# A hybrid decoder step on one core: DVE's queue in program order, a third buffer for projected tiles, one buffer for gate and square

## Chip, core, metric

One core of a Trainium2 chip. The metric is the device time of one execution in microseconds (us). Engines: PE (TensorE; PEld is its weight load), DVE (VectorE), ACT (ScalarE), POOL (GpSimd), SP (SyncE, which issues most transfers).

## What is computed

One layer of a decoder with two parallel groups of eight heads, all in float32, for 512 new tokens of a prompt and for 8 sequences with 4 new tokens each (32 tokens), so T = 544 columns in all. Cut to what matters:

```python
p = einsum('btd,de->bte', rmsnorm(x), w_in)          # 2048 -> 8192 columns
qa, ka, va, za, qb, fb, ib, zb = split(p)            # 1024 columns each
# group A, per head: stick-breaking attention; causal means s < t
z = qa @ ka.T * scale + bias
log_1m = where(causal, log_sigmoid(-z), 0)
tail = reverse_cumsum(log_1m) - log_1m
o_a = where(causal, exp(log_sigmoid(z) + tail), 0) @ va
# group B, per head: gated linear recurrence
g = lb + (1 - lb) * sigmoid(fb)
S_t = diag(g_t) S_{t-1} + (1 - g_t) ib_t^T ;  o_b_t = S_t^T silu(qb_t)
# both
m = concat(head_rmsnorm(o_a) * silu(za), head_rmsnorm(o_b) * silu(zb))
y = rmsnorm(x + m @ w_out)
```

The 8 sequences attend besides to 2048 cached positions each, in pages of 128, and start group B from a stored state. Keys, values and states of the new tokens are outputs too.

## The kernel before

**Product with split weights.** Each float32 weight piece (128 x 1024 values) is loaded by SP, rounded by ACT (`whi`, L259) and its remainder taken by DVE (`wlo`, L260). `project` (L381) multiplies a column block of 128 by all tokens in three products (hi x hi, hi x lo of the tokens, lo x hi), 96 matmuls for two pieces, into two PSUM banks (the whole pool `ps_acc`), one for each half of the tokens. At the end DVE empties each half into a tile in SBUF (L408). The next projection begins in the bank of the first half. These tiles come from `atile` (L924), with AT buffers.

**Order of the work.** `Flow` (L76) decides while the program is written: the base work is the sequence of projections, in portions of four matmuls; between portions it inserts side work (attention, decoding of pages, recurrence) from generators, each of which names the cost of its next step, the delay until it may come, and how long it holds one of three PSUM banks (`GBANKS`, `gbank`). The delays and the hold are numbers written by hand. When a step is inserted, its instructions for all engines are issued, so that the program has one order in which each engine's instructions stand. Under `manual_schedule` (L164) PE and SP keep that order in their queues. The queues of DVE, ACT and POOL are put in order by the scheduler of the framework, which lets an instruction pass others that it believes to be waiting still; once built, each queue is fixed.

**Stages.** Token tiles are transposed and split first (`prep_tokens`); at portion 23 of the first projection that is over (L944) and the pools for the rest are opened. Then come the eight query projections of group A; then `group_a`: for each head K, V and gate projections, with `attend` (L455) of the head beside the gate's projection. In `attend`, for each of four token blocks (512, 384, 256 and 128 columns): a score matmul into a bank (zp, L462); DVE empties it (L464); POOL masks the diagonal (L465); then `stick_sums`:

```python
nc.scalar.activation(lt[:, :n], z[:, :n], AF.Exp)                     # L447
nc.scalar.activation(lt[:, :n], lt[:, :n], AF.Ln, bias=1.0)           # L448
nc.vector.scalar_tensor_tensor(lt[:, :n], z[:, :n], GUARD, lt[:, :n], # L449
                               ALU.max, ALU.min)
nc.vector.tensor_tensor_scan(...)                                     # L450
nc.vector.tensor_tensor(z[:, :n], z[:, :n], lt[:, :n], ALU.subtract)  # L452
```

After the four blocks PE transposes K and V into banks (knp, vnp, and kvsp for the 32 new tokens), which ACT (L478) and DVE (L487, L489) empty; later steps transpose the weights of attention (wp) and multiply them by V (op). `gate` (L411) computes a sigmoid in three ACT passes (L217 to L219) and two products on DVE (L413, L414). `finish_head` (L416) squares the output on POOL (L418, tile sq), sums the squares with two matmuls (L425, L426), takes the root on ACT, and scales on DVE (L429, L436); the result goes to DRAM from the buffer of sq (L437).

`decode` (L645) runs beside both groups in 36 steps: pages of keys are loaded by SP (kpage, three buffers), transposed by DVE (L550, `k_turn`, the second of a step 14 us of planned time after the first) and multiplied (dzp, L678); pages of values are multiplied by the weights (av, L688). After every fourth step the scores of a sequence go through L698 and `stick_sums`.

`group_b`: for each head the projections bq, bf, bi and, mostly behind them, bz; `hgrn` (L705) is added when bi is written. It makes operands on DVE (L711 to L717), then goes through four rounds: two pairs of score matmuls (L746), selected into att (L757 to L763 in the first round, six L803 and in one round L811 in the others), and operands for the next round (L818, L822, L779, L781). Then transposes (khp, khsp), states and outputs. At last `out_first` and `out_rest` multiply by w_out (yacc, L1106).

**Buffers that the change touches.** In `atile` two buffers serve q, K, V and gate tiles in turn, in `group_b` bq, bf, bi and bz. `hgrn` reads q (L711) only after bi was written. In group A the gate uses a tile sg of 544 columns and `finish_head` a tile sq of 512; in group B the sigmoids of `hgrn` and of the gate share a tile sgm, and sq is another.

Of the kernel before, what the change touches and what calls it, by code (L numbers as in the profile page):

```python
# [9 lines left out]
F32 = mybir.dt.float32  # L10
# [8 lines left out]
P = 128  # L19
D = 2048  # L20
NK = D // P
SEQ = 512
# [4 lines left out]
T = SEQ + NS  # L27
# [113 lines left out]
def hybrid_step(ctx: ExitStack, tc: tile.TileContext, x_prompt, x_sample, cache_k, cache_v, state_s, page_table,  # L141
# [27 lines left out]
    def gbank(name):  # L169
        return ps_g.tile([P, 512], F32, name=name, tag="g")  # L170
# [7 lines left out]
    def mm(n):  # L178
        return 4.0 * max(n, 128) / 2.4
# [31 lines left out]
    def rsqrt_mean(out, ssq, n):  # L211
        k = out.shape[0]
        nc.scalar.activation(out, ssq, AF.Ln, bias=eps[:k], scale=1.0 / n)
        nc.scalar.activation(out, out, AF.Exp, scale=-0.5)

    def sigmoid(out, x):
        nc.scalar.activation(out, x, AF.Exp, scale=-1.0)  # L217
        nc.scalar.activation(out, out, AF.Ln, bias=1.0)
        nc.scalar.activation(out, out, AF.Exp, scale=-1.0)  # L219
# [191 lines left out]
    def gate(hh, zt, sg):  # L411
        sigmoid(sg, zt)
        nc.vector.tensor_tensor(zt[:, :SEQ], zt[:, :SEQ], sg[:, :SEQ], ALU.mult)  # L413
        nc.vector.tensor_tensor(sz_s[:, hh, :], zt[:, SEQ:], sg[:, SEQ:], ALU.mult)  # L414

    def finish_head(pool, hh, ot, zt, after):  # L416
        sq = pool.tile([P, SEQ], F32, name="sq", bufs=1)
        nc.gpsimd.tensor_tensor(sq, ot, ot, ALU.mult)  # L418
        hi = pool.tile([P, SEQ], F32R, name="sqhi", bufs=1)
        lo = pool.tile([P, SEQ], F32R, name="sqlo", bufs=1)  # L420
        nc.scalar.activation(hi, ot, AF.Square)
        nc.gpsimd.tensor_tensor(lo, sq, hi.bitcast(F32), ALU.subtract)
        yield mm(512) / 2, after + 2500.0, 1500.0, 0.0
        sp = gbank("sp")
        nc.tensor.matmul(sp, ones_r, hi, start=True, stop=False)  # L425
        nc.tensor.matmul(sp, ones_r, lo, start=False, stop=True)  # L426
        rs = sq
        rsqrt_mean(rs, sp, P)
        nc.vector.scalar_tensor_tensor(rs, ot, gains[:, hh:hh + 1], rs, ALU.mult, ALU.mult)  # L429
        if hh >= KEPT:  # L430
            while dec_done[0] < DB:
                yield 0.0, 500.0, 0.0, 0.0
            m_raw[hh] = dp.tile([P, SEQ], F32, name="vpage", bufs=NV)
            nc.vector.tensor_tensor(m_raw[hh], rs, zt[:, :SEQ], ALU.mult)
        else:
            nc.vector.tensor_tensor(rs, rs, zt[:, :SEQ], ALU.mult)  # L436
            nc.gpsimd.dma_start(m_dram[hh], rs)  # L437
        m_done[hh] = True

    KEPT = 14  # L440
    OFF = 7000.0
    AT = 2
    m_done = [False] * 16
    m_raw = [None] * 16

# [9 lines left out]
    def attend(h, qt, kt, vt, res):  # L455
# [56 lines left out]
        if "zt" in res:  # L512
            yield from finish_head(ap, h, ot, res["zt"], 1500.0)
# [20 lines left out]
    def k_fetch(n):  # L534
        while len(kpending) < min(n, len(kunits)):
            t = dp.tile([P, 4, 512], F32, name="kpage", bufs=3)
            b, gp, h2 = kunits[len(kpending)]
            for i in (0, 2, 1, 3):
                src = kpages[page_value(k_held, b, gp, i), :, h2 * 512:h2 * 512 + 512]
                nc.sync.dma_start(t[32 * i:32 * i + 32], src.rearrange("o (s r) e -> (o r) s e", r=32))  # L540
            kpending.append(t)
# [161 lines left out]


    def hgrn(h, q, F, it, res):  # L705
        sg = bp_.tile([P, T], F32, name="sgm")
        sigmoid(sg, q)
        e0 = etile()
        e3 = e0[:, :3 * T // 2].rearrange("p (u x) -> p u x", x=3)
        pairs = "p (u t) -> p u t"  # L710
        nc.vector.tensor_tensor(e3[:, :, 0:2], q.rearrange(pairs, t=2), sg.rearrange(pairs, t=2), ALU.mult)  # L711
        sg = bp_.tile([P, T], F32, name="sgm")
        sigmoid(sg, F)
        nc.vector.tensor_scalar(F, sg, lb1[:, h:h + 1], lb0[:, h:h + 1], ALU.mult, ALU.add)
        f2 = F.rearrange(pairs, t=2)
# [173 lines left out]
        if finish:  # L889
            yield from finish_head(bp_, H + h, ot, res["zt"], 1500.0)  # L890
# [33 lines left out]
    def atile(name):  # L924
        return tp_.tile([P, T], F32, name=name, tag="at", bufs=AT)

    def group_a():
        nonlocal ap, dp, tp_, later, earlier
        for h in range(H):
            if h == H - 1:  # L930
                k_fetch(3)
            if h == 2:
                for c in (slice(0, 6 * P), slice(6 * P, NM * P)):
                    lvlf = ap.tile([P, 6 * P], F32, name="lt", tag="lvlf", bufs=1)[:, :c.stop - c.start]
                    nc.gpsimd.dma_start(lvlf, masks[:, c])
                    nc.gpsimd.tensor_copy(lvls[:, c], lvlf)
            qts = []

            def qtile():
                qts.append(atile("qt"))  # L940
                return qts[0]

            for i, c in enumerate(project(qtile, h * P, h == 0)):
                if h == 0 and i == 23:  # L944
                    flow.wait(lambda: not flow.side)
                    xstack.close()
                    dp = dstack.enter_context(tc.tile_pool(name="dpool", bufs=1))
                    dcon = dp.tile([P, C_TOT - C_LATER], F32, name="dcon")
                    nc.sync.dma_start(dcon, consts[:, C_LATER:])
                    later, earlier = dcon[:, :P], dcon[:, P:]  # L950
                    tp_ = dstack.enter_context(tc.tile_pool(name="tpool", bufs=1))
                    lvls = tp_.tile([P, NM * P], U8, name="lvls")
                    lvl.extend(lvls[:, P * i:P * i + P] for i in range(NM))
                    ap = astack.enter_context(tc.tile_pool(name="apool", bufs=1))
                yield c
            nc.gpsimd.tensor_copy(q_new[:, h, :], qts[0][:, SEQ:])
            nc.gpsimd.dma_start(q_dram[h], qts[0][:, :SEQ])
        flow.add(decode(H / 64, STOP), 2)
        for h in range(H):
            qt = ap.tile([P, SEQ], F32, name="ql", bufs=2)  # L960
            nc.sync.dma_start(qt, q_dram[h])
            kt = atile("kt")
            yield from project(kt, W + h * P)
            vt = atile("vt")
            yield from project(vt, 2 * W + h * P)
            res = {}
            flow.wait(lambda: not a_side or a_side[-1] not in flow.side)
            a_side.append(flow.add(attend(h, qt, kt, vt, res), 0))
            zt = atile("zt")
            yield from project(zt, 3 * W + h * P)  # L970
            sg = ap.tile([P, T], F32, name="sg")
            gate(h, zt, sg)
            res["zt"] = zt
            if "ot" in res:
                a_side.append(flow.add(finish_head(ap, h, res["ot"], zt, 4500.0), 0))
# [31 lines left out]
    def group_b():  # L1007
        ress = [{} for _ in range(H)]

        def heads(h):  # L1010
            q = atile("bq")
            yield from project(q, 4 * W + h * P)
            F = atile("bf")
            yield from project(F, 5 * W + h * P)
            if h:
                flow.wait(lambda: hg_done[h - 1])
            if not h:
                open_b()
            it = atile("bi")
            yield from project(it, 6 * W + h * P)  # L1020
            flow.add(hgrn(h, q, F, it, ress[h]), 0)

        def gates(h):
            zt = atile("bz")
            yield from project(zt, 7 * W + h * P)
            sg = bp_.tile([P, T], F32, name="sgm")
            gate(H + h, zt, sg)
            ress[h]["zt"] = zt
            if "ot" in ress[h]:
                flow.add(finish_head(bp_, H + h, ress[h]["ot"], zt, 4500.0), 0)  # L1030

        for h in range(H - 1):
            yield from heads(h)
            if h < H - 2:
                yield from gates(h)
        yield from heads(H - 1)
        for c in gates(H - 2):
            load_m()
            yield c
        flow.wait(lambda: merged)  # L1040
        load_m()
        flow.add(mix_first, 1)
        yield from gates(H - 1)

    def load_m():
        if dec_done[0] < DB or not all(m_done[:KEPT]) or m_raw[0] is not None:
            return
        for k in (0, 4):
            t = dp.tile([P, 4, 512], F32, name="kpage", bufs=3)
            nc.sync.dma_start(t, m_dram[k:k + 4].rearrange("k p t -> p k t"))  # L1050
            for j in range(4):
                m_raw[k + j] = t[:, j, :]
        for k in range(8, KEPT):
            m_raw[k] = dp.tile([P, SEQ], F32, name="vpage", bufs=NV)
            nc.sync.dma_start(m_raw[k], m_dram[k])
# [213 lines left out]
```

## Time and profile before

| | us |
|---|---|
| timed runs, median of 2 | 1408.0 (1407.3 and 1408.7) |
| the profiled execution | 1405.46 |
| its span, first to last instruction | 1403.8 |
| PE busy | 1331.7 |
| DVE busy | 758.3 |
| ACT busy | 413.6 |
| POOL busy | 311.7 |

The span is the time between the first and the last instruction that the profiler recorded; the execution takes 1.7 us more. Busy time is the union of an engine's instructions. Matmuls are pipelined, so PE's busy time is not PE at its peak. In a row, "a <-b" behind a number tells what ended the idle time before an instruction.

### The profile page before, as it was taken

The numbers are of one execution on the slowest core, as the hardware profiler recorded it, in microseconds if no ns is written. First come the engines' busy times: TensorE is split into PE (matmuls) and PEld (weight loads), VectorE is DVE, ScalarE is ACT, GpSimd is POOL, SyncE is SP. The second block draws the span as 40 slices with busy tenths as digits, with TensorE's granted clock in tenths as the row PEclk, the third lists the DMA queues.
The fourth block names the chain that finished last, engine by engine and source line by source line (L and its number), as shares of the span: only waits on it lengthen the run. The fifth ranks groups of instructions, "written<-read, shape, count | busy, mean of one in ns | idle before, by whom it ended". The sixth has DMA issues, their size and how long they took to land.

```text
span 1403.8 us, 30662 instructions
## 1 busy us (share of the span) xinstructions
PE 1331.7 (95%) x11922; PEld 1215.2 (87%) x11922; DVE 758.3 (54%) x1302; ACT 413.6 (29%) x701; POOL 311.7 (22%) x577
## 2 busy tenths in 40 slices
PE   6999999899999999999989989999999999999997
PEld 6999888798988888888887978889899897988996
DVE  6324555647466474667575674665455658222223
ACT  6211324224233242331222231132323225222223
POOL 3212113112132121132332232121213324111001
PEclk9999999999999999999999999999999999999999
DMA  7338876699989898898888978746523251622223
GB/s 218 109 109 214 200 203 163 174 292 235 280 228 269 236 258 220 229 273 212 247 231 233 274 193 235 229 143 196 149 61 113 65 194 42 240 76 78 89 76 143
DMA packets 245027, 260.69 MB, mean 186 GB/s; under 512 B 13497, under 2 KB 169842, under 8 KB 244178
## 3 DMA queue, kind: packets, MB, share of 16 engines
q1 hardware_dynamic: 237600, 235.00, 60.5%
q0 software_dynamic: 5504, 15.80, 3.3%
q10 hardware_dynamic: 1778, 7.93, 1.5%
q8 instruction: 94, 1.54, 0.5%
q14 instruction: 51, 0.42, 0.1%
HBM read 239.15 MB, written 19.53 MB: 184 GB/s over the span
## 4 chain that ended last, share of the span: by engine, by line
PE 74%; issue 10%; DVE 9%; DMA 3%; ACT 3%; POOL 1%; SPq 0%; DVEq 0%; POOLq 0%; ACTq 0%
PE pacc L401 42%; PE yacc L1106 13%; DVE kpage L550 3%; PE av L688 3%; PE dzp L678 3%; PE sp L746 2%; DMA kpage<-in_cache_k 2%; PE op L507 1%; PE usp L897 1%; PE ysp L1115 1%; DVE wlo L260 1%; DMA wraw<-in_w_in 1%; DVE lt L450 1%; DVE att L803 1%; PE wp L174 1%
## 5 line engine op out<-in xcount | busy, mean ns | idle before, releaser
L401 PE MATMUL pacc<-h_hi,whi 128*128 128x256 f32 (+1 forms) x2048 | 546.4, 299 | 15.2 <-ACT whi L259 9.8
L401 PE MATMUL pacc<-h_lo,whi 128*128 128x256 f32 (+1 forms) x2048 | 530.4, 289 | 0.0
L401 PEld LDWEIGHTS pacc<-h_hi,whi 128*128 128x128 f32 x2048 | 389.1, 190 | 40.1 <-issue 22.9
L401 PEld LDWEIGHTS pacc<-h_lo,whi 128*128 128x128 f32 x2048 | 389.2, 190 | 1.7 <-issue 0.2
L260 DVE TENSOR_TENSOR wlo<-wraw,whi 128x1024 fp32r<-128x1024 f32 x160 | 198.0, 1240 | 199.0 <-PE yacc L1106 78.0
L259 ACT CAST whi<-wraw 128x1024 fp32r<-128x1024 f32 x160 | 166.6, 1046 | 458.3 <-PE pacc L401 312.7
L401 PE MATMUL pacc<-h_hi,wlo 128*128 128x256 f32 (+1 forms) x2048 | 294.6, 292 | 0.0
L401 PEld LDWEIGHTS pacc<-h_hi,wlo 128*128 128x128 f32 x2048 | 269.5, 189 | 13.0 <-issue 12.3
L550 DVE STREAM_TRANSPOSE kpage<-kpage 128x2048 f32<-128x2048 f32 x64 | 146.2, 2296 | 0.2 <-issue 0.2
L1106 PE MATMUL yacc<-whi,m_hi 128*128 128x256 f32 x512 | 130.4, 293 | 0.0
L1106 PE MATMUL yacc<-whi,m_lo 128*128 128x256 f32 x512 | 126.7, 285 | 3.1 <-DVE m_lo L1096 3.0
L1106 PEld LDWEIGHTS yacc<-whi,m_hi 128*128 128x128 f32 x512 | 98.8, 193 | 16.8 <-issue 13.0
L1106 PEld LDWEIGHTS yacc<-whi,m_lo 128*128 128x128 f32 x512 | 99.1, 194 | 3.6 <-DVE m_lo L1096 3.5
L678 PE MATMUL dzp<-kpage,qblk 128*32 128x128 f32 x2048 | 68.3, 281 | 23.1 <-DVE kpage L550 23.0
L678 PEld LDWEIGHTS dzp<-kpage,qblk 128*32 128x32 f32 x2048 | 54.8, 112 | 33.0 <-DVE kpage L550 27.4
L1106 PE MATMUL yacc<-wlo,m_hi 128*128 128x256 f32 x512 | 68.3, 282 | 0.0
L1178 POOL TENSOR_TENSOR y<-y,fnw 128x512 f32<-128x512 f32 (+1 forms) x18 | 26.3, 1477 | 178.7 <-DVE y L1174 111.2
L1106 PEld LDWEIGHTS yacc<-wlo,m_hi 128*128 128x128 f32 x512 | 64.3, 191 | 0.0
L688 PE MATMUL av<-vpage,dwt 128*32 128x512 f32 x512 | 62.2, 600 | 0.0
L658 POOL COPY qblk<-q_new 32x32 f32<-32x32 f32 x128 | 45.7, 357 | 31.0 <-PE dzp L678 25.8
L746 PE MATMUL sp<-bE,kr 128*128 128x192 f32 x256 | 47.4, 326 | 1.9 <-DVE o_s L596 1.4
L803 DVE COPY_PREDICATED att<-lvls,sp 128x192 f32<-128x192 uint8 (+2 forms) x144 | 38.3, 310 | 15.9 <-PE sp L746 14.9
(262 smaller groups left out, 1372.3 us busy)
## 6 DMA issues: line engine op xcount, KB each, us to landing
wraw<-in_w_in SPq DMA_DIRECT2D x128, 512.0 KB, 5.9
kpage<-in_cache_k SPq DMA_DIRECT2D x256, 256.0 KB, 5.5
vpage<-in_cache_v SPq DMA_DIRECT2D x256, 256.0 KB, 5.1
wraw<-in_w_out SPq DMA_DIRECT2D x32, 512.0 KB, 3.5
bst<-in_state_s SPq DMA_DIRECT2D x16, 256.0 KB, 6.2
out<-bst POOLq DMA_DIRECT2D x16, 256.0 KB, 3.9
y<-in_x_prompt ACTq DMA_DIRECT2D x4, 1024.0 KB, 7.4
xt<-in_x_prompt SPq DMA_DIRECT2D x7, 512.0 KB, 5.8
```

The lines of the kernel that those rows point to most:

```text
L174: nc.tensor.transpose(out, in_, ident[:k, :k])
L259: turns.append(nc.scalar.copy(hi, raws[i]))
L260: nc.vector.tensor_tensor(lo, raws[i], hi.bitcast(F32), ALU.subtract)
L401: nc.tensor.matmul(ps[half][:, :n], a[:, j, :], x[:, j, ts], start=(kh == 0 and part == 0 and r == 0), stop=(kh == 1 and part == 1 and r = ...
L550: nc.vector.transpose(flat, flat)
L658: nc.gpsimd.tensor_copy(out.rearrange("p h (g x) -> p h g x", g=4)[:, :, :, :DT], q_new[32 * j:32 * j + 32, :, DT * b:DT * b + DT].rearran ...
L678: nc.tensor.matmul(zp[32 * g:32 * g + 32, gp * P:(gp + 1) * P], qb[:, at:at + 32], kt[:, g, :, 32 * j:32 * j + 32], start=(gp == 0 and h2 ...
L688: nc.tensor.matmul(av[hf][32 * i:32 * i + 32, :], wt[:, gp, i, :], vpending[n], start=(gp == 0), stop=(gp == 3))
L746: nc.tensor.matmul(sp[:, i * 192:(i + 1) * 192], kr[:, n * P:(n + 1) * P], moving(n), start=True, stop=True)
L803: nc.vector.copy_predicated(a4[:, :, :, d * hl:], m.unsqueeze(1).to_broadcast([P, 2, u, w]), s4[:, :, :, at:at + w])
L1106: nc.tensor.matmul(out, m[4 * kq + j][:, c], b[:, j, :], start=(kq == 0 and part == 0 and r == 0 and (one or tb % 2 == 0)), stop=(kq == 3 ...
L1178: nc.gpsimd.tensor_tensor(part, part, fnw[:, cs].unsqueeze(1).to_broadcast([P, n, CG]), ALU.mult)
```

## The change

It opens a second region in which DVE, too, keeps the program's order; it begins where the token tiles are done and lasts to the end. It gives `atile` three buffers. It lets sq and the sigmoids' tiles share one buffer in each of the two groups.

```diff
     def finish_head(pool, hh, ot, zt, after):
-        sq = pool.tile([P, SEQ], F32, name="sq", bufs=1)
+        sq = pool.tile([P, T], F32, name="sq", tag="sg", bufs=1)[:, :SEQ]
         nc.gpsimd.tensor_tensor(sq, ot, ot, ALU.mult)
...
-    AT = 2
+    AT = 3
...
     def hgrn(h, q, F, it, res):
-        sg = bp_.tile([P, T], F32, name="sgm")
+        sg = bp_.tile([P, T], F32, name="sgm", tag="sg")
         sigmoid(sg, q)
...
-        sg = bp_.tile([P, T], F32, name="sgm")
+        sg = bp_.tile([P, T], F32, name="sgm", tag="sg")
         sigmoid(sg, F)
...
                     xstack.close()
+                    ctx.enter_context(tc.manual_schedule(engines={mybir.EngineType.DVE}))
                     dp = dstack.enter_context(tc.tile_pool(name="dpool", bufs=1))
...
         def gates(h):
...
-            sg = bp_.tile([P, T], F32, name="sgm")
+            sg = bp_.tile([P, T], F32, name="sgm", tag="sg")
             gate(H + h, zt, sg)
```

## Rows read from the trace of the kernel before

**Rows 1.** The page, part 1: busy us, share, instructions.

```profile
PE 1331.7 (95%) x11922; PEld 1215.2 (87%) x11922; DVE 758.3 (54%) x1302; ACT 413.6 (29%) x701; POOL 311.7 (22%) x577
```

**Rows 2.** Windows: stretch, length, busy by engine (instructions), PEclk, DMA share, GB/s.

```profile
150.00:570.00 420.00, 390.32 (x3817) 354.05 (x3816) 249.45 (x358) 139.99 (x256) 86.22 (x168) 0.98 0.85 229
570.00:920.00 350.00, 332.27 (x3276) 297.94 (x3278) 222.56 (x412) 89.95 (x139) 85.98 (x192) 0.99 0.84 231
920.00:1175.00 255.00, 251.43 (x1929) 232.62 (x1917) 144.04 (x341) 72.34 (x102) 68.06 (x135) 0.99 0.42 127
```

**Rows 3.** Waits of PE: line, whom for, us in total, times, longest.

```profile
PE dzp L678 <- DVE kpage L550: 23.0, 15, 3.4
PE pacc L401 <- ACT whi L259: 9.8, 4, 3.5
...
PE knp L174 <- DVE z L464: 2.8, 2, 1.9
PE pacc L401 <- DVE zt L408: 2.4, 1, 2.4
```

**Rows 4.** Timeline of DVE, third head of group A: start, us, instruction, [idle before].

```profile
265.80 0.75 DVE L464 TENSOR_SCALAR z<-zp,sbb 128x512 f32<-128x512 f32 x1 [1.76 <-PE zp L462]
268.34 0.69 DVE L449 SCALAR_TENSOR_TENSOR lt<-z,lt 128x512 f32<-128x512 f32 x1 [1.79 <-ACT lt L448]
269.07 1.23 DVE L450 TENSOR_TENSOR_SCAN lt<-ones_r,lt 128x512 f32<-128x512 f32 x1
270.33 0.69 DVE L452 TENSOR_TENSOR z<-z,lt 128x512 f32<-128x512 f32 x1
270.93 1.22 DVE L260 TENSOR_TENSOR wlo<-wraw,whi 128x1024 fp32r<-128x1024 f32 x1
```

**Rows 5.** Groups by line and shape, 150 to 570 us: busy, mean ns | idle.

```profile
L464 DVE TENSOR_SCALAR z<-zp,sbb 128x128 f32<-128x128 f32 x8 | 2.7, 343 | 0.0
L450 DVE TENSOR_TENSOR_SCAN lt<-ones_r,lt 128x128 f32<-128x128 f32 x8 | 3.2, 398 | 0.0
...
L447 ACT ACTIVATE lt<-z 128x512 f32<-128x512 f32 x8 | 5.0, 630 | 78.9 <-POOL z L465 78.9
L447 ACT ACTIVATE lt<-z 128x128 f32<-128x128 f32 x8 | 2.4, 295 | 0.0
```

**Rows 6.** Timeline, second head of group A, DVE and PE.

```profile
207.88 0.61 DVE L464 TENSOR_SCALAR z<-zp,sbb 128x384 f32<-128x384 f32 x1
...
208.54 0.71 PE L174 MATMUL knp<-cst,kt 128*128 128x128 f32 x4 [1.93 <-DVE z L464]
```

**Rows 7.** Timeline, first and last head of group A: first L464 and kvsp.

```profile
154.14 0.75 DVE L464 TENSOR_SCALAR z<-zp,sbb 128x512 f32<-128x512 f32 x1 [1.35 <-PE zp L462]
...
159.67 0.27 PE L174 MATMUL kvsp<-cst,kt 128*32 128x128 f32 x1
...
556.66 0.75 DVE L464 TENSOR_SCALAR z<-zp,sbb 128x512 f32<-128x512 f32 x1 [1.35 <-PE zp L462]
...
560.10 0.27 PE L174 MATMUL kvsp<-cst,kt 128*32 128x128 f32 x1
```

**Rows 8.** Timeline, third head of group B, DVE, then PE.

```profile
802.69 1.45 DVE L803 COPY_PREDICATED att<-lvls,sp 128x192 f32<-128x192 uint8 x6
...
813.10 0.69 DVE L449 SCALAR_TENSOR_TENSOR dc<-dz,dc 128x512 f32<-128x512 f32 x1 [1.36 <-ACT dc L448]
...
815.69 2.30 DVE L550 STREAM_TRANSPOSE kpage<-kpage 128x2048 f32<-128x2048 f32 x1
...
805.09 0.35 PE L401 MATMUL pacc<-h_hi,whi 128*128 128x256 f32 x1 [0.56 <-DVE bz L408]
...
813.21 1.46 PE L746 MATMUL sp<-bE,kr 128*128 128x192 f32 x8
...
819.79 0.91 PE L174 MATMUL khp<-cst,kr 128*128 128x128 f32 x4 [2.67 <-DVE att L803]
```

**Rows 9.** Windows: a stretch of the second head of group A.

```profile
200.00:225.00 25.00, 20.64 (x191) 18.68 (x189) 19.45 (x29) 9.96 (x22) 12.88 (x26) 0.93 0.82 207
```

## The prediction

> **What bounds the kernel now.** I read the page first. PE is busy for 1331.7 us of a span of 1403.8, 95% [rows 1], so whatever PE loses is lost by the kernel, and whatever it cannot lose is safe. DVE is busy for about half of the time. Cutting the span into stages [rows 2] shows where PE's 72 us of idle time lie: 29.7 in the attention stage (420 minus 390.32, from 150 to 570 us), 17.7 in the recurrent stage while cached pages are still read (350 minus 332.27), 3.6 in the rest of that stage; start and end hold most of what is left. The waits of PE [rows 3] give the causes: 23.0 us for key pages that DVE has not yet transposed, 9.8 for weights that ACT has not yet rounded, 2.8 and 2.4 for a PSUM bank and an accumulator that DVE has not yet emptied. All of it is order on DVE and ACT, none of it their total work. So at most some 45 us can be won (29.7 + 17.7, less what has other causes), and the question is whether the program's order serves PE better than the planner's.
>
> **What changes on DVE.** No operation is added or removed. Before, DVE's queue was ordered by the scheduler, which let an instruction pass others that were waiting. Afterwards each DVE instruction stands exactly where the Python code issues it. That hurts where the code issues a chain that leaves DVE for ACT and comes back: DVE now waits out the round trip.
>
> **Term 1, attention: four chains one behind another.** For every head, attend issues per token block one score matmul into a PSUM bank, then on DVE L464 (which empties the bank), L449, L450 and L452, with POOL and two ACT passes between L464 and L449. Four blocks of 512, 384, 256 and 128 columns follow one another. In one head of before the first chain happened to run unmixed [rows 4]: L464 at 265.80, L449 only at 268.34 after 1.79 us idle, and the next DVE instruction at 270.93. So one chain of 512 columns holds DVE for 5.2 us. A chain of 128 columns is shorter by 0.41 on L464 and 0.83 on L450 (0.75 and 1.23 [rows 4] against 0.343 and 0.398 [rows 5]), by twice 0.335 for the ACT passes (630 against 295 [rows 5]) and, as an estimate, by as much as L464 on L449 and on L452: 5.2 minus 2.7 is 2.5. In thirds between: 4.3 and 3.4.
>
> There are three banks for such work. The fourth score matmul takes the first chain's bank, then the transposes knp, vnp and kvsp take the banks of chains 2, 3 and 4, which are free when the L464 of each is done. That this is a real wait is seen in [rows 6]: knp began at 208.54 after 1.93 us idle, right after the second L464 (207.88 plus 0.61). In program order those L464 end at 5.2 + 0.6 = 5.8, at 5.2 + 4.3 + 0.5 = 10.0 and at 5.2 + 4.3 + 3.4 + 0.3 = 13.2 us after the first one starts. PE does not pass a waiting instruction, so kvsp starts 13.2 us after the first L464. In before it starts 5.5 us after it in the first head (159.67 minus 154.14) and 3.4 in the last (560.10 minus 556.66) [rows 7]; over the eight heads 5.5, 9.3, 10.1, 3.5, 3.5, 3.9, 3.4 and 3.4, in all 42.6. The loss is 8 x 13.2 minus 42.6 = 63 us. In the first two heads a wait for rounded weights of about 2.5 us comes just after (part of the 9.8 of [rows 3]) and now falls into the longer one: 58. Bounds: 0, if DVE's slack took it all, and 85, if POOL and ACT make each chain a fifth longer (8 x 2.7 more). I take 58, since the chain and the bank wait are both rows of this kernel.
>
> A rule of the Trainium skill speaks the other way here (Perfetto Trace Analysis, Optimizing Tensor Performance): independent matmul groups should rotate through PSUM banks, so that emptying one overlaps the next. By it three banks cover this and term 1 is nothing, which would take the sum below from 1495 to 1437. The row with 1.93 us shows the rotation already stopping PE in before.
>
> **Term 2, the recurrent heads.** Here the chain of a round is: scores on PE, six L803, then L818, L822, L779 and L781, which make the operands of the next round. Before, the scheduler put some of these last ones, the emptying of an accumulator (L408) and a key transpose ahead of others. I walked one head in program order with the durations of [rows 8]. PE issued the first scores of the round at 801.31, so L803 can start at 802.05; with six L803, L811, L818 (0.68), L822, L779 and L781 (0.5, 0.4, 0.3) ahead of it, L408 ends at 806.5 and PE resumes there, not at 805.09: 1.5 us. Then come the transpose (2.3), L408's other half (0.4), three ACT passes for the gate (2.1) with DVE waiting, L413 and L414 (0.8), a weight remainder L260 (1.2, [rows 4]), L803 and the four operand makers (3.4): ready at 816.7. PE has 8.1 us of work from its resumption to the third round (813.21 minus 805.09) and wants it at 814.7: 2 more. If a decode chain stands behind it (L698 to L452, 4.8 us with 1.36 idle), then another transpose (2.3), six L803, L818 and L822 (2.7), khp starts at 826.4 and not at 819.79: 6.6 us for that head. Without the decode chain the sum is 1.5 + 2 = 3.5. Four heads have pages beside them: 4 x 5 = 20. In the last four there is no transpose; the same walk gives 1.9 for L408 alone and 3 with the gate, two heads each: 10. Term 2 is 30. Bounds: minus 5 (the 3.6 us of idle there and little more, if everything fits) and 60 (two such waits per head).
>
> **Term 3, what is won.** A key transpose that the scheduler moved behind chains now stands where the code has it. Of the 23.0 us [rows 3] I give back half, 12; bounds 0 and 23.
>
> **Term 4, the clock.** After idle time PE ran for a while at half speed: 0.93 granted over 25 us [rows 9] is 3.5 us at 1.2 instead of 2.4 GHz, which costs 1.7 us. Six such stretches lie in 150 to 920 us. With gaps of 3.8, 3.2 and 2.7 us in every attention head I add four there and two later: 11 us with the lost work of the longer ones. Bounds 0 and 25.
>
> **The two other edits.** Three buffers instead of two for projected tiles: with DVE in program order the third tile of a recurrent head could not be written before q is read, and q is read behind it, so two would not do. It shortens nothing that PE waits for: no wait of PE for such a tile's reader is in [rows 3]. One buffer for gate and square: the square of a head (POOL) waits for the gate's last reader, and a sigmoid waits for the store of the head before. The planner puts the matmul that needs the square 7 us behind the gate, more than the wait; without that cover it would cost a round trip like the 1.79 of [rows 4] for up to sixteen heads, 29 us. I take 0.
>
> **Sum.** The profiled execution took 1405.5 us; 58 + 30 - 12 + 11 = 87 more is 1492.5. The median of the timed runs is 2.5 us above that execution: 1495.
>
> **Rivals.**
> - Attention alone pays, DVE's slack swallows term 2: 58 - 12 + 8 = 54 more, 1462. For it: DVE is free for half of the recurrent stage. Against: its operands are made in a chain.
> - ACT starves PE as well: the rounding of the next weights sits in ACT's queue behind the last chain's exponentials, and PE waits another 4 us in every attention head: 32 more, 1527. For it: the 9.8 us of [rows 3] arose so.
> - It is faster: the order costs nothing because PE finds a free bank, and late transposes, unrounded weights and clock losses go. All of them (23.0 + 9.8 + 2.8 + 2.4 and six times 1.7) are 48; half is 24: 1384. It decides if knp starts within some 2 us of the first L464, as it did in five heads. Against it stands the program's own order.
> - It makes no difference, because DVE is not what limits: 1408. A reorder of an engine with 46% of its time free would then be absorbed. This is the Trainium skill's rule (Perfetto Trace Analysis, Identifying the Most-Contended Engine): work on the engine with the highest occupancy first; by it DVE at 54% moves nothing.
> - It doesn't do what it says, because the region opened inside the outer one ends PE's and SP's own order; no row prices that.
>
> **Chances and range.** The forecast 0.50, attention alone 0.20, ACT too 0.14, faster 0.07, no difference 0.07, not as said 0.02 (put with no difference). About 2%, 28 us, can be told from no change. So slower 0.84, within 2% 0.09, faster 0.07. The range goes from 1430 (attention alone with half of term 1: 1408 + 29 - 12 + 4) to 1560 (ACT too, with term 1 at its upper bound: 1527 + 27, and a little more); the forecast's own is 1460 to 1530.
>
> **What would show it.** Right: in every attention head DVE runs L464, L449, L450, L452 four times over with 1 to 2 us idle in each; PE waits for L464 before knp, vnp and kvsp, some 9 us a head and 60 or more in all; PE's idle time between 150 and 570 us roughly triples; L408 and L822 appear among PE's waits in the recurrent stage; the wait for key transposes shrinks. Wrong: knp within 2 us of the first L464, or PE's wait for L464 staying under 10 us in all, or a recurrent stage as dense as before.

## The result: 9% slower, and the profile after

The changed kernel takes 1538.5 us (median of two runs, 1535.4 and 1541.6) against 1408.0: 1.093 times the time of before, 95% interval 1.083 to 1.102. Slower was forecast and the time lies in the range, but the forecast was 87 us more and it is 130. The profiled execution took 1541.6 us, its span is 1539.9. Lines of the changed kernel behind L947 are one higher than before.

Part 1 of the page after, which answers to [rows 1]:

```profile
PE 1381.2 (90%) x11922; PEld 1252.5 (81%) x11922; DVE 776.2 (50%) x1302; ACT 423.5 (28%) x701; POOL 303.8 (20%) x577
```

The instructions are the same in number. PE's idle time went from 72.1 us (1403.8 minus 1331.7) to 158.7, by 86.6; and PE is *busy* for 49.5 us longer with the same matmuls. So the 136 us have two parts, and the second is not a wait.

Windows of the changed kernel by stage: attention (from the first emptying of a key tile to that of the first bq), the recurrent heads (to the last bz), the end. Columns as in [rows 2].

```profile
139.60:675.60 536.00, 454.21 (x4155) 409.26 (x4154) 273.34 (x376) 159.27 (x271) 83.01 (x172) 0.91 0.72 195
675.60:1299.30 623.70, 573.22 (x4939) 518.21 (x4941) 358.65 (x737) 152.38 (x223) 146.95 (x322) 0.96 0.62 172
1299.30:1539.90 240.60, 224.24 (x1817) 198.95 (x1816) 85.53 (x102) 68.82 (x147) 41.24 (x28) 0.95 0.31 108
```

The same three stages of the kernel before, cut at its own marks:

```profile
139.30:595.10 455.80, 426.12 (x4154) 388.05 (x4153) 268.16 (x375) 148.74 (x270) 91.08 (x172) 0.99 0.85 230
595.10:1173.50 578.40, 557.78 (x4940) 507.07 (x4942) 351.82 (x738) 153.10 (x224) 149.30 (x324) 0.99 0.66 186
1173.50:1403.80 230.30, 219.63 (x1816) 195.45 (x1810) 79.35 (x102) 68.73 (x147) 37.61 (x27) 0.98 0.33 113
```

Attention pays 80.2 us, of which 52.1 idle (81.8 minus 29.7) and 28.1 more busy time; the recurrent heads 45.3, of which 29.9 idle and 15.4 busy; the end 10.3 (5.7 and 4.6). The granted clock fell from 0.99 to 0.91 and 0.96, and that is the longer busy time: up to PE's last matmul, the clock record of the trace of before has 9 stretches at 1.2 GHz, 37.5 us in all, that of the changed kernel 27, 160.4 us in all. PE was busy for 35.8 and 124.6 us of them. Half of the 88.8 us more is 44, of the 49.5 (an estimate: work at half speed taken to last twice as long).

The waits of PE in the changed kernel's attention stage, then in its recurrent stage; they answer to [rows 3]:

```profile
PE knp L174 <- DVE z L464: 28.5, 8, 4.1
PE dzp L678 <- DVE kpage L550: 15.6, 4, 6.2
PE pacc L401 <- DVE kt L408: 12.0, 2, 9.5
PE pacc L401 <- DVE vt L408: 6.3, 1, 6.3
...
PE sp L746 <- DVE bE L781: 12.0, 5, 4.9
PE khp L174 <- DVE kr L822: 9.7, 4, 4.3
PE pacc L401 <- DVE bz L408: 8.8, 7, 1.9
```

Every one of these is a wait for DVE, which is busy half of the time. What DVE itself waits for, first after, then before:

```profile
DVE wlo L260 <- ACT whi L259: 118.6, 26, 10.0
...
DVE lt L449 <- ACT lt L448: 63.7, 32, 4.5
```

```profile
DVE wlo L260 <- ACT whi L259: 25.0, 10, 4.7
...
DVE lt L449 <- ACT lt L448: 6.1, 8, 1.8
```

The 32 waits at L449 are the 8 x 4 chains of term 1. The 118.6 us at L260 stand in no term: the code writes the low part of a weight piece (L260) a piece ahead, and DVE stops there until ACT has rounded it, with all that is due behind it. The scheduler had placed it where the wait was short.

The clearest place is at 464 us, DVE's timeline of the changed kernel:

```profile
464.34 1.23 DVE L260 TENSOR_TENSOR wlo<-wraw,whi 128x1024 fp32r<-128x1024 f32 x1 [9.51 <-ACT whi L259]
465.48 0.74 DVE L429 SCALAR_TENSOR_TENSOR sq<-ot,vecs,sq 128x512 f32<-128x512 f32 x1
...
468.97 0.69 DVE L449 SCALAR_TENSOR_TENSOR dc<-dz,dc 128x512 f32<-128x512 f32 x1 [1.36 <-ACT dc L448]
469.70 1.22 DVE L450 TENSOR_TENSOR_SCAN dc<-ones_r,dc 128x512 f32<-128x512 f32 x1
470.96 0.69 DVE L452 TENSOR_TENSOR dz<-dz,dc 128x512 f32<-128x512 f32 x1
471.57 2.30 DVE L550 STREAM_TRANSPOSE kpage<-kpage 128x2048 f32<-128x2048 f32 x1
473.79 0.38 DVE L596 TENSOR_REDUCE o_s<-detp 128x4 f32<-128x16 f32 x4
474.10 0.77 DVE L408 TENSOR_TENSOR kt<-pacc,rbc 128x256 f32<-128x256 f32 x2
```

The accumulator that PE needs was full by 464.7; it is emptied at 474.10, behind a wait for a weight, a decode chain that waits for ACT, and a page. PE's timeline at that place:

```profile
474.65 0.55 PE L401 MATMUL pacc<-h_hi,whi 128*128 128x256 f32 x1 [9.52 <-DVE kt L408]
475.00 0.41 PE L401 MATMUL pacc<-h_lo,whi 128*128 128x256 f32 x1
475.21 0.41 PE L401 MATMUL pacc<-h_hi,whi 128*128 128x256 f32 x1
...
484.34 0.28 PE L401 MATMUL pacc<-h_lo,whi 128*128 128x256 f32 x1
484.46 0.28 PE L401 MATMUL pacc<-h_hi,whi 128*128 128x256 f32 x1
```

And the windows around it, 10 us each:

```profile
465.00:475.00 10.00, 0.48 (x3) 0.38 (x2) 8.54 (x15) 1.51 (x3) 0.59 (x1) 0.76 1.04 312
475.00:485.00 10.00, 10.00 (x63) 10.00 (x63) 2.60 (x11) 2.22 (x5) 1.16 (x2) 0.73 0.38 102
485.00:495.00 10.00, 10.00 (x130) 8.19 (x129) 7.36 (x6) 1.05 (x1) 0.00 (x0) 1.00 0.36 101
```

From 475 to 485 us PE waits for nothing, but the clock is at 0.73: some 5.4 of the 10 us went by at 1.2 instead of 2.4 GHz. In them matmuls of one and the same shape start 0.21 us apart, and 0.12 us afterwards. As an estimate, 5.4 us at 0.12/0.21 of the pace lose some 2.3 us, and this gap of 9.5 us cost about 12. The counts, 63 and 130 matmuls, don't give the loss: the second stretch has 64 short ones of a key page among them, which take 2 us.

### The profile page after: what moved, and what is told of

Read it like the earlier page. It is cut to its first block, busy times and chain, and to the rows that moved or that the text cites. A ratio compares the mean times of both kernels' runs of the same rounds, so it can differ in the third digit from the quotient of the medians.

```text
span 1539.9 us, 30643 instructions
## 1 busy us (share of the span) xinstructions
PE 1381.2 (90%) x11922; PEld 1252.5 (81%) x11922; DVE 776.2 (50%) x1302; ACT 423.5 (28%) x701; POOL 303.8 (20%) x577
## 5 line engine op out<-in xcount | busy, mean ns | idle before, releaser
L401 PE MATMUL pacc<-h_hi,whi 128*128 128x256 f32 (+1 forms) x2048 | 561.9, 305 | 32.7 <-DVE kt L408 12.0
L401 PE MATMUL pacc<-h_lo,whi 128*128 128x256 f32 (+1 forms) x2048 | 543.5, 295 | 0.0
L401 PEld LDWEIGHTS pacc<-h_hi,whi 128*128 128x128 f32 x2048 | 400.8, 196 | 57.9 <-issue 46.5
L401 PEld LDWEIGHTS pacc<-h_lo,whi 128*128 128x128 f32 x2048 | 400.7, 196 | 1.9 <-issue 0.5
L260 DVE TENSOR_TENSOR wlo<-wraw,whi 128x1024 fp32r<-128x1024 f32 x160 | 204.4, 1279 | 282.3 <-ACT whi L259 118.6
L401 PE MATMUL pacc<-h_hi,wlo 128*128 128x256 f32 (+1 forms) x2048 | 298.1, 294 | 0.0
L401 PEld LDWEIGHTS pacc<-h_hi,wlo 128*128 128x128 f32 x2048 | 273.5, 192 | 14.6 <-issue 14.0
L550 DVE STREAM_TRANSPOSE kpage<-kpage 128x2048 f32<-128x2048 f32 x64 | 147.1, 2300 | 0.0
L678 PE MATMUL dzp<-kpage,qblk 128*32 128x128 f32 x2048 | 68.9, 288 | 23.4 <-DVE kpage L550 23.4
L688 PE MATMUL av<-vpage,dwt 128*32 128x512 f32 x512 | 65.6, 633 | 0.0
L746 PEld LDWEIGHTS sp<-bE,kr 128*128 128x128 f32 x256 | 43.2, 198 | 15.1 <-issue 14.2
L803 DVE COPY_PREDICATED att<-lvls,sp 128x192 f32<-128x192 uint8 x144 | 42.4, 314 | 19.3 <-PE sp L746 16.0
```

Source lines behind the costliest of these rows:

```text
L260: nc.vector.tensor_tensor(lo, raws[i], hi.bitcast(F32), ALU.subtract)
L401: nc.tensor.matmul(ps[half][:, :n], a[:, j, :], x[:, j, ts], start=(kh == 0 and part == 0 and r == 0), stop=(kh == 1 and part == 1 and r = ...
L550: nc.vector.transpose(flat, flat)
L678: nc.tensor.matmul(zp[32 * g:32 * g + 32, gp * P:(gp + 1) * P], qb[:, at:at + 32], kt[:, g, :, 32 * j:32 * j + 32], start=(gp == 0 and h2 ...
L688: nc.tensor.matmul(av[hf][32 * i:32 * i + 32, :], wt[:, gp, i, :], vpending[n], start=(gp == 0), stop=(gp == 3))
L746: nc.tensor.matmul(sp[:, i * 192:(i + 1) * 192], kr[:, n * P:(n + 1) * P], moving(n), start=True, stop=True)
```

## The experiments

The theory: in a fixed queue each instruction that waits for ACT holds back what PE is waiting for, at several separate places, and every gap on PE costs half-speed time besides. Rivals: the buffers, losses carried from one stage to the next, a wait that only moves. The stages of all kernels, from their windows as above; in each pair the first number is the length, the second PE's idle time in it (length minus PE busy), in us. The median is that of all timed runs; stages and PE busy are those of the one profiled execution, which in *attention only* was the slowest (1498.1) and in *recurrent on* the quickest (1458.0).

| kernel | median | ratio to before, 95% | attention | recurrent | end | PE busy |
|---|---|---|---|---|---|---|
| before | 1408.0 | | 455.8, 29.7 | 578.4, 20.6 | 230.3 | 1331.7 |
| changed | 1538.5 | 1.083 to 1.102 | 536.0, 81.8 | 623.7, 50.5 | 240.6 | 1381.2 |
| buffers only | 1410.2 | 1.000 to 1.004 | 459.0, 29.5 | 579.5, 22.9 | 229.9 | 1331.4 |
| attention only | 1491.2 | 1.053 to 1.063 | 539.2, 80.1 | 585.0, 22.4 | 229.8 | 1371.8 |
| recurrent on | 1466.0 | 1.037 to 1.046 | 458.0, 29.5 | 621.3, 49.3 | 237.9 | 1348.6 |
| chains held | 1500.0 | 1.061 to 1.071 | 493.9, 55.8 | 621.1, 47.9 | 240.5 | 1363.1 |
| operands first | 1529.6 | 1.084 to 1.090 | 534.3, 79.5 | 611.6, 42.2 | 240.3 | 1377.1 |
| low part later | 1494.4 | 1.059 to 1.065 | 510.4, 63.6 | 604.2, 38.8 | 237.9 | 1362.3 |
| three together | 1441.7 | 1.021 to 1.026 | 475.5, 38.3 | 590.2, 31.8 | 236.1 | 1343.0 |
| five together | 1434.9 | 1.016 to 1.024 | 469.3, 38.1 | 589.9, 27.7 | 232.9 | 1343.2 |
| five, order free | 1413.8 | 1.003 to 1.007 | 461.7, 30.3 | 579.2, 21.3 | 232.3 | 1339.0 |

**Buffers only.** The line that fixes DVE's order is left out.

```diff
-                    ctx.enter_context(tc.manual_schedule(engines={mybir.EngineType.DVE}))
```

> The two buffer edits alone: three buffers for projected tiles, gate and square in one buffer, and DVE's order left to the scheduler again, as before. Theory (DVE's fixed order costs everything): 1408 us within 0.5%, PE's idle gaps and half-speed stretches as before (63.5 us and 42.9 us). Rival (the buffers carry part of the loss: the shared buffer holds the next gate back until the head's square is done, and the third tile lets projections run ahead of the side work): 1420 us or more, with waits of ACT's sigmoid for POOL or DVE on that buffer.

Measured 1410.2, PE busy 1331.4. By themselves the buffers carry at most 0.4%; the rest of the loss comes with the line that is left out. The shared buffer does leave a wait: the sigmoids of group B (L217) wait 27.0 us in all for the store of a head's result (`m_dram`) from it, and 33.7 us in the changed kernel. PE's idle time in the recurrent stage is 2.3 us above that of before here; whether the wait costs more while DVE's order is fixed was not run.

What that line changes, the traces of this kernel and of the changed one show, by line and tile of each instruction: PE's 11922 matmuls and SP's transfers stand in the same order in both. Of DVE's 1302 instructions at least 450 stand elsewhere. So do at least 160 of ACT's 701 and 119 of POOL's 577, though their queues are still the scheduler's: it ordered them anew around DVE's. No run separates what ACT's new order adds to the waits of DVE for ACT.

**Attention only, and from the recurrent heads on.** The region is closed, or opened, just ahead of group B (`mstack` is a new `ExitStack`).

```diff
-                    ctx.enter_context(tc.manual_schedule(engines={mybir.EngineType.DVE}))
+                    mstack.enter_context(tc.manual_schedule(engines={mybir.EngineType.DVE}))
...
+    mstack.close()
     flow.run(group_b(), per=2)
```

> The changed kernel, with DVE's fixed order closed where the recurrent heads begin. Theory (each stage pays for its own queueing): the attention stage keeps its 80 us (first key tile to first recurrent query tile 536 us instead of 456), the recurrent stage is as before (about 578 us for the recurrent heads, 230 us for the end): 1408 + 80 = 1488 us. Rival (attention leaves pages and decode work late, and that is what costs the recurrent heads their 45 us): the recurrent stage is still 30 us or more longer than before, 1520 us or more.

```diff
-                    ctx.enter_context(tc.manual_schedule(engines={mybir.EngineType.DVE}))
...
+    ctx.enter_context(tc.manual_schedule(engines={mybir.EngineType.DVE}))
     flow.run(group_b(), per=2)
```

> The changed kernel, with DVE's fixed order opened only where the recurrent heads begin. Theory (each stage pays for its own): attention as before, recurrent heads +45 us, the end +10 us: 1408 + 55 = 1463 us. Rival (the recurrent loss is carried over from attention): the recurrent heads lose less than 15 us, 1420 us.

Measured 1491.2 and 1466.0. With the region closed the recurrent stage is 585.0 us long (6.6 over before), with the region opened late it is 621.3. Both rivals fall: each stage pays for itself, and the two losses, 5.8% and 4.1%, add up to that of the changed kernel (9.3%, interval 8.3 to 10.2).

**Chains held.** The second half of a chain is written one block later, behind the next block's L464; `exp_log` is the two ACT passes, `chain` what follows them, and the last block's is written behind the transposes of K.

```diff
-            stick_sums(z, lt, n)
-            nc.scalar.activation(z, z, AF.Exp)
+            exp_log(z, lt, n)
+            for due in held:
+                due()
+
+            def due(z=z, lt=lt, n=n):
+                chain(z, lt, n)
+                nc.scalar.activation(z, z, AF.Exp)
+
+            held = [due]
```

> The changed kernel, with the second half of each attention chain (max, scan, subtraction) written one block later, behind the next block's eviction of its scores, so that no eviction in DVE's queue has a chain in front of it that waits for ACT. Theory (the written order, not the fixing of it, costs the attention heads): PE's waits of the natural-key bank for L464 fall from 28.5 us to under 6, the attention stage gets shorter by these and by a share of the half-speed clock (28 of 86 us of gaps brought about 16 of 50 us): about 1495 us. Rival (the wait moves: the same chains then stand in front of the key tile, the decode chain and the pages): within 1% of 1538 us, with those waits grown by as much.

DVE's timeline in the last head of this kernel (L470 is L464 of before, L455 to L458 are L449 to L452):

```profile
589.65 1.27 DVE L470 TENSOR_SCALAR z<-zp,sbb 128x512 f32<-128x512 f32 x2
592.46 0.69 DVE L455 SCALAR_TENSOR_TENSOR lt<-z,lt 128x512 f32<-128x512 f32 x1 [1.54 <-ACT lt L448]
...
595.06 0.48 DVE L470 TENSOR_SCALAR z<-zp,sbb 128x256 f32<-128x256 f32 x1
```

Two banks are emptied at once, and the group "knp waits for L464" (28.5 us) is no longer among PE's waits; in all, PE waits 2.8 us for kvsp's bank. The attention stage is 42.1 us shorter, 26.0 of it idle time and 16.1 busy time. The wait did not move (that for key pages fell from 23.4 to 18.0 us in the whole kernel, that of zp for L464 from 6.1 to 5.2), and the three banks were enough.

**Operands first.** In the recurrent rounds the products for the next round are written ahead of the masked copies of the first half, the keys ahead of those of the second (`next_tile` holds L818, L779 and L781, `next_keys` L822; their definitions, and the first round's, which is changed likewise, are left out here).

```diff
             def finish(half, sp):
+                (next_keys if half else next_tile)()
                 u = P // (4 * hl)
```

> The changed kernel, with the recurrent heads' operands written ahead of the masked copies: the next round's products (L818, L779, L781) before the copies of the first half of a round's scores, the next keys (L822) before those of the second half. Theory (PE waits there because the copies L803, which nobody waits for, stand in front of the operands): sp's wait for L781 and khp's for L822 (12.0 and 9.7 us) fall under 5 together, and the recurrent heads get shorter by these 17 us and their share of the half-speed clock: about 1515 us. Rival (the score banks, which then come free later, and the gate in front of the round take their place): within 0.5% of 1538 us.

Measured 1529.6, less than half of the gain, and not clear of the spread: its interval lies inside that of the changed kernel. The recurrent stage is 12.1 us shorter, 8.2 of it idle time. Waits of PE in the recurrent stage of this kernel (L817 is the keys' line, L822 of before):

```profile
PE sp L746 <- DVE kr L817: 9.3, 4, 4.2
PE khp L174 <- DVE kr L817: 6.6, 3, 4.1
```

The wait for the products is gone and the keys end it instead, nearly as late: 15.9 us instead of 21.7. The copies were only part of what stood in front. Ahead of the longest of these waits of sp, which ends at 914.7 us, DVE waits 2.17 us for the gate's sigmoid and 3.04 at L260; ahead of that of khp (924.4 us) stand a decode chain and a page.

**Low part later.** L260 of a piece is written when the piece before it begins its last third (`low_parts` writes what is due; in `out_block` likewise). The first four pieces and the last four are left as they were.

```diff
-            nc.vector.tensor_tensor(lo, raws[i], hi.bitcast(F32), ALU.subtract)
+            late.append(lambda r=raws[i], lo=lo, hi=hi: nc.vector.tensor_tensor(lo, r, hi.bitcast(F32), ALU.subtract))
...
         taken[0] += 1
+        low_parts()
         split_ahead(i + 2)
...
             n = ts.stop - ts.start
+            if part == 1:
+                low_parts()
             if part == 0:
```

> The changed kernel, with the low part of each weight piece (L260) written half a piece later (some 6 us, still ahead of the piece that uses it). Theory (L260 stands in DVE's queue and waits there for ACT's rounded copy while evictions behind it are due): PE's waits for the key and value tiles' L408 (12.0 and 6.3 us) go, about 18 us of gaps and 10 us of clock: about 1510 us. Rival (the eviction is late because of the decode chain in front of it, whatever L260 does): those two waits stay above 10 us together and the time is within 0.7% of 1538 us.

Measured 1494.4, 44 us less than the changed kernel: the largest part found, in both stages (25.6 and 19.5 us), and more than expected. Waits of PE in the attention stage (L419 is L408, L561 is L550 of before):

```profile
PE dzp L689 <- DVE kpage L561: 11.4, 3, 5.5
PE pacc L412 <- ACT whi L259: 8.1, 2, 7.3
PE pacc L412 <- DVE kt L419: 3.6, 2, 2.9
...
PE pacc L412 <- DVE vt L419: 0.5, 1, 0.5
```

The key and value tiles' waits went from 18.3 us to 4.1. A new one came, 8.1 us for weights not yet rounded by ACT.

**Three together, and five.** The three rewritings; then with two more: the decode chain behind its eviction by some microseconds, and the last gate behind the low parts of the first eight mixed heads.

> The three rewritings together: attention chains held back by a block, operands ahead of the masked copies, the low weight parts half a piece later, all with DVE in the written order. Theory (they are separate waits that add): 1538 less 39 less 23 less 28, about 1448 us, still slower than before by the page transposes and decode sums. Rival (one takes the place of the other): 1480 us or more.

> The three rewritings and two more of the same kind, DVE in the written order: the decode chain (max, scan, subtraction of the 512 cached keys) written a little later than its eviction, so that the page transposes and masked copies behind it don't wait for ACT; and the last gate written behind the low parts of the first eight mixed heads. Theory (each such wait costs its own gap and about half as much again in clock): the waits of 7.4 us (detp for a masked copy), 4.3 us (khp) and 4.1 us (yacc for m_lo) go, some 16 us of gaps: 1442 - 24 = 1418 us. Rival (what is left is the late weights and pages, which the written order can't mend): 1435 us or more.

```diff
-                stick_sums(z, ct, 512)
+                exp_log(z, ct, 512)
...
     def weigh(b, z, ct):
-        yield 2 * 430.0, OFF, 1000.0, 0.0
+        yield 0.0, 3000.0, 0.0, 0.0
+        chain(z, ct, 512)
+        yield 2 * 430.0, OFF - 3000.0, 1000.0, 0.0
...
             split_m(k)
+        last_gate[0]()
         banks = [bank(t, "yacc") for t in PAIRS[0]]
```

Three together: 1441.7, where the single gains (38.5, 8.9 and 44.1) would give 1447. They add to within some 5 us, so they are in the main separate waits. The other two brought 7 us, not 24, and the two intervals overlap: the end got shorter by 3.2 us and the waits for a masked copy and for khp went down, but PE's idle time fell by 9.6 us and not by 16, one new wait of 3.5 us appeared, and the busy time stayed. The largest waits of the last kernel (L412 is L401, L576 is L550 of before):

```profile
PE pacc L412 <- ACT whi L259: 13.6, 3, 8.5
PE dzp L706 <- DVE kpage L576: 12.0, 5, 4.5
PE pacc L412 <- DVE bz L419: 8.0, 7, 2.1
```

Of that run the rival was nearer: late weights and pages are what is left. Why ACT's rounding is late there was not pursued.

**Five, order free.** The line that fixes DVE's order is left out of the kernel with five.

> The same five rewritings, DVE's order left to the scheduler. Theory (the scheduler already issues what is ready, whatever the written order): the time of before, 1408 us within 1%. Rival (the written order is also the scheduler's order of preference, and the old one was good for it): 1425 us or more.

Measured 1413.8, 0.5% over before. With the scheduler's order the rewritings neither help nor hurt much. No version beat the kernel before.

## Why the prediction was right and where it was not

**Right: the sign, the mechanism and, in sum, the idle time.** The measured time is inside the whole range (1430 to 1560), but outside the forecast's own (1460 to 1530), and nearer to the 1527 of "ACT too" than to 1495. Terms 1 to 3 came to 76 us of lost time, and PE's idle time grew by 86.6. Four chains of L464, L449, L450 and L452 follow one another in each head, and knp started 5.8 us after the first L464 in all eight heads, as worked out. Attention alone costs 83 us, not the 54 of that rival; DVE's slack swallowed nothing of term 2, which was put at 30 and showed 29.9 us of idle time: 16.7 in the four heads with pages (put at 20) and 13.2 in the others (10). In attention, terms 1 and 3 together came to 46 and the idle time grew by 52.1; that these are close is in part luck, since both terms were wrong, as told below, and a wait that was in neither made up for it.

**Wrong, and the main miss: term 4, the clock.** It was put at 11 us with a bound of 25; PE's busy time grew by 49.5. The step that failed is the count and the length of the half-speed stretches: six more, most as short as the 3.5 us of [rows 9]. There were eighteen more (27 instead of 9), 123 us in all (160.4 minus 37.5), and in 88.8 us of that PE had work. Behind the gap at 475 us alone, PE worked for about 5.4 us at 1.2 GHz. With 49.5 in its place the sum would have been 1405.5 + 76 + 49.5 + 2.5 = 1533.5.

**Wrong in its parts: term 1.** vnp and kvsp were to wait for the L464 of chains 3 and 4. They did not. PE's timeline in the seventh head of the changed kernel:

```profile
559.42 1.11 PE L174 MATMUL knp<-cst,kt 128*128 128x128 f32 x4 [3.61 <-DVE z L464]
561.29 1.05 PE L174 MATMUL vnp<-cst,vt 128*128 128x128 f32 x4
563.02 0.29 PE L174 MATMUL kvsp<-cst,kt 128*32 128x128 f32 x1 [0.68 <-ACT vn L478]
```

They went on with the banks that ACT had emptied. kvsp began 9.0 to 12.0 us after the first L464, in all 79.2 over eight heads instead of 105.6, so this loss is 79.2 minus 42.6, 37 us and not 63 (58 after what was taken off). What filled the difference was not in the sum: above all L260 in front of the key and value tiles, for which PE waited 18.3 us. *Chains held* made the attention stage 42 us shorter and *low part later* 26, so both are real.

**Wrong: term 3.** The wait for key pages did not shrink: 23.0 us in [rows 3], 23.4 in the changed kernel (15.6 and 7.8). A page now stands behind all four chains: DVE's timeline in the fifth head.

```profile
429.45 0.29 DVE L452 TENSOR_TENSOR z<-z,lt 128x128 f32<-128x128 f32 x1
429.67 2.30 DVE L550 STREAM_TRANSPOSE kpage<-kpage 128x2048 f32<-128x2048 f32 x1
```

PE had waited for it since 426.6. The code's place for a transpose was no better than the scheduler's.

**Not in the sum: the end.** 10.3 us, 5.7 of it idle. PE's waits for m_lo, the low parts of the mixed heads, went from 3.0 to 8.0 us. *Low part later* brought them to 5.3 and the stage down by 2.7 us. In the changed kernel these parts stand behind the last gate, which waits 3.1 us for a sigmoid; with the gate behind them (*five together*) PE waited 0.9 us for m_lo and the stage was 3.2 us shorter than in *three together*. The end was costed at nothing because the walk stopped at the recurrent heads.

**The two buffers.** Costed at 0, measured at 0.2% (interval 0.0 to 0.4) with the scheduler's order. The sigmoid's wait for the store, which the prediction named, is there (33.7 us in the changed kernel). What the buffers cost while DVE's order is fixed, and that two for projected tiles would not do then, was not tried.

**The rivals.** "ACT starves PE as well" had the right engine and the wrong path: PE's own wait for ACT's rounding fell from 9.8 to 1.0 us; ACT's lateness reached PE through DVE, which waited for it at L260. "It is faster" fell: knp began within 2 us of the first L464 in no head. "It makes no difference" fell: DVE's busy share is 50%, and the loss is 9%. The rule of the Trainium skill (Perfetto Trace Analysis, Identifying the Most-Contended Engine) to optimize first the engine with the highest occupancy, taken as that rival took it, would have misled: PE is the busiest by far here, and what slowed it down was the order on an engine at half load. "It doesn't do what it says" fell: PE and SP kept their order to the last instruction. The other rule that was weighed (the same page, Optimizing Tensor Performance), that rotating banks hide the emptying, holds here under a condition: with three banks the wait was 28.5 us when the emptying stood behind chains in DVE's queue, and gone in *chains held* with the same three.

**What stays open.** The span of *three together* is still 37.0 us longer than that of before, 25.7 of it idle and 11.3 busy time of PE; which written order would take the waits for pages and weights out as well was not found.

## What to carry to other kernels

Fixing the order of an engine's queue makes every instruction that waits for another engine hold back all that stands behind it, so first look in the written order for chains that leave the engine and return, and for work written ahead of its operands; write the emptying of PSUM ahead of both. List every instruction of the queue that waits, not only those of the step under study: the dearest one here (L260) was in no term. And price a gap on PE above its length: in this kernel the span grew by about one and a half times the idle time.

## What was not expected of the hardware

How regular the price of PE's gaps is. Against before, the spans of the eight slower kernels grew by 1.4 to 1.8 us for each us of idle time added on PE: 136.1 for 86.6 (changed), 92.6 for 52.5 (attention only), 52.5 for 35.6 (recurrent on), 92.4 for 61.0 (chains held), 124.1 for 78.7 (operands first), 87.5 for 56.9 (low part later), 37.0 for 25.7 (three together), 27.6 for 16.1 (five together), each from one profiled execution. The rest is PE's own busy time, which was 1343 to 1381 us with the same 11922 matmuls (1331.7 before). It is the longer, by and large, the more the kernel stopped, but not strictly: *attention only* has less idle time than *chains held* (124.6 and 133.1 us) and more busy time (1371.8 and 1363.1).
